# One hybrid diffusion step on one core: modulation matmuls kept in runs, and an opening stage that takes two output chunks a step

## Chip, core and metric

The kernel runs on one core of a Trainium2 chip. The time is device microseconds of one execution. PE is TensorE, DVE is VectorE, ACT is ScalarE, POOL is GpSimd, and SP issues most of the DMA.

## What is computed

Two layers run over 128 context tokens and 128 latent tokens, which the kernel carries side by side as 256 columns. Cut to what matters here:

```python
def _modulation(cond, w_mod, b_mod):
    m = jax.nn.silu(cond) @ w_mod + b_mod            # (2048) @ (2048, 6 * 2048)
    return [t[:, None, :] for t in jnp.split(m, 6, axis=-1)]

def _layer(x, mods, lw, ctx):
    shift1, scale1, gate1, shift2, scale2, gate2 = mods
    h = _rms_norm(x, lw['norm1_g']) * (1.0 + scale1) + shift1
    parts = _split_cols(h @ lw['w_in'])              # GLA, attention, DeltaNet heads
    mix = mixers(parts) @ lw['w_out']
    x = x + gate1 * mix
    h = _rms_norm(x, lw['norm2_g']) * (1.0 + scale2) + shift2
    ff = jnp.square(jax.nn.relu(h @ lw['w_ff1'])) @ lw['w_ff2']
    return x + gate2 * ff
```

There are two conditioning vectors (context and latent), so each of the six modulation slices of a layer is a product of a 2048 x 2048 float32 weight with two columns.

## The kernel before

Every weight comes from HBM in float32 tiles `raw` of 128 x 1024 (512 KB). For a dense product ACT rounds it to `hi` and DVE subtracts to get `lo`; PE then multiplies hi by the rounded activations `act`, hi by their remainder, and lo by the rounded part. The buffer of a `raw` comes free when `lo` is made. For a modulation slice no split is made: `sc`, the two conditioning columns, is the stationary operand, 32 columns wide, and the `raw` tile streams past it in float32. A float32 matmul is two instructions in the trace, so counts there are doubled. Since `sc` fills only 32 columns, four such matmuls go to the four column groups of the array (`tile_position=(0, 32 * gg)`), and each writes its own 32 rows of one PSUM bank.

`mod_pe` makes a slice outside the opening: 16 steps of two `raw` and four matmuls of 512 columns. Six slices go this way: 384 matmuls, or 96 groups of four. Four more slices are made on DVE (`mod_dv`), and slices 0 and 1 of layer 0 belong to the opening.

`first_phase` is the opening. It sums the squares of x on ACT and DVE, gets `rstd`, and then walks 16 output chunks n of 128. A chunk makes shift1 and scale1 for its 128 features: four `raw`, sixteen matmuls of 256 columns into the one bank of pool `pmod`, ACT copies it to `msb`, PE selects with `sel2` into a second tile of the same pool (`mod0t`), DVE adds the bias and makes `s12` and `ht`, and ACT and DVE write act[:, n]. For n below 8 the chunk of the input projection that act[:, n] allows is added to fourteen accumulators in seven PSUM banks (`fb`, `fbm`, `fbn`; weights `w_in0`, 896 columns a part). For n from 8 the step gives out a share of `half_jobs`: the first half of three more units (`HALF_D`, into `g`) and of three token units (`HALF_T`, into `gt`). All `raw` tiles of the opening come from the six buffers of pool `raw0`. After the opening the loop over `FIRST` adds the second half, with `raw` from the six buffers of `wraw`.

The order on each engine is not the order of the code. A scheduler simulates the program when it is built and writes a fixed order per engine; a token given to matmuls (`tok`) makes those that share it keep the order of the code among themselves. On the chip each engine goes through its order, and one instruction that waits holds all behind it. SP does the same with DMA issues.

Of the kernel before, what the change touches and what calls it, by code (L numbers as in the profile page):

```python
# [10 lines left out]
F32 = mybir.dt.float32  # L11
# [5 lines left out]
P = 128  # L17
# [1 line left out]
EPS = 1e-6  # L19
LEVELS = (16, 32, 64)  # L20
FIRST = (12, 0, 1, 2, 3, 4, 5, 6, 7, 8, 9, 10, 11, 13)
HALF_D = (14, 15, 16)
HALF_T = (0, 1, 2)
TB = 4
NRAW = 6
# [15 lines left out]
def tile_hybrid_step(ctx: ExitStack, tc: tile.TileContext, A: dict, O: dict):  # L41
# [381 lines left out]

    def mod_pe(l, m, modc, bm):
        ps = pmod.tile([P, 512], F32, tag="mod", name="mod")
        for k in range(16):
            raws = [load_half(A["w_mod"][l, m, k, half]) for half in range(2)]
            for gg in range(4):
                mm(
                    ps[32 * gg : 32 * gg + 32, :],  # L430
                    sc[:, 2 * k : 2 * k + 32],
                    raws[gg // 2][:, (gg % 2) * 512 : (gg % 2) * 512 + 512],
                    start=(k == 0),
                    stop=(k == 15),
                    tile_position=(0, 32 * gg),
                )
            yield
        msb = nrm.tile([P, 512], F32, tag="msb", name="msb")
        se.activation(msb, ps, AF.Copy)
        pt = ps  # L440
        for r in range(4):
            mm(pt[:, r * 8 : r * 8 + 8], msb[:, r * P : r * P + P], sel8)
        ve.tensor_tensor(
            modc[:, m].rearrange("p (g r) c -> p r g c", r=4),
            pt[:, 0:32].rearrange("p (r g c) -> p r g c", r=4, c=2),
            bc(bm[:, m].rearrange("p (g r) -> p r g", r=4), 2),
            ALU.add,
        )
        yield
# [16 lines left out]
    def get_rstd():  # L466
        st = pm.tile([P, 512], F32, tag="m", name="st")
        for g in range(2):
            mm(st[:, g : g + 1], sqacc[:, g * P : g * P + P], ones[:, 0:1])
        np_ = X["np"]  # L470
        v = np_.tile([P, 2], F32, tag="nv", name="nv")
        ve.tensor_scalar(v, st[:, 0:2], 1.0 / 2048.0, EPS, ALU.mult, ALU.add)
        rs = newton(np_, v, 2, "n2")
        b = bcast_cols(np_, rs, 2, "ht", 2)
        rstd = np_.tile([P, 256], F32, tag="rstd", name="rstd")
        se.activation(rstd, b[:, 0:256], AF.Copy)
        return rstd
# [70 lines left out]
    def first_phase(raw0):  # L548
        modc, s12, bm, ng = mods[0]
        X["np"] = raw0  # L550
        for n in range(16):
            accum_sq(n, n == 0)
        rate[0] = 0
        rstd = get_rstd()
        nb = len(FIRST)
        banks = [pg.tile([P, 512], F32, tag="g", name="fb") for _ in range(2)]
        banks += [pm.tile([P, 512], F32, tag="m", name="fbm") for _ in range(3)]
        banks += [pn.tile([P, 512], F32, tag="m", name="fbn") for _ in range(2)]
        tok = newtok()

        def half_jobs():
            for j in HALF_D:
                def evac(ps, j=j):
                    se.activation(part_of(j), gq3(ps), AF.Copy)

                yield from gemm_pieces(tsrc(A["w_in"][0], j), (0,), lambda k: act[:, k, 0:512], evac, raw0)
            for u in HALF_T:
                yield from gemm_tok(
                    lambda q, u=u: A["w_tok"][0][u, q], range(4),
                    lambda ps, g, u=u: se.activation(tok_dest(u, g), ps, AF.Copy), raw0,  # L570
                )

        jobs = half_jobs()
        njobs = 3 * len(HALF_D) + 12 * len(HALF_T)
        done = 0
        for n in range(16):
            ps = pmod.tile([P, 512], F32, tag="mod", name="mod0")
            for q in range(4):
                raw = load_half(A["w_mod0"][n, q], raw0)
                for kk in range(4):  # L580
                    mm(ps[32 * kk : 32 * kk + 32, 0:256], sc[:, 2 * (4 * q + kk) : 2 * (4 * q + kk) + 32], raw[:, kk * 256 : kk * 256 + 256],
                       start=(q == 0), stop=(q == 3), tile_position=(0, 32 * kk))
            msb = nrm.tile([P, 512], F32, tag="msb", name="msb")
            se.activation(msb[:, 0:256], ps[:, 0:256], AF.Copy)
            pt = pmod.tile([P, 512], F32, tag="mod", name="mod0t")
            for m in range(2):
                mm(pt[:, 2 * m : 2 * m + 2], msb[:, m * P : m * P + P], sel2)
            ve.tensor_tensor(
                modc[:, 0:2, n, :], pt[:, 0:4].rearrange("p (m c) -> p m c", m=2), bc(bm[:, 0:2, n], 2), ALU.add
            )  # L590
            ve.tensor_scalar(s12[:, 0, n, :], modc[:, 1, n, :], 1.0, ng[:, 0, n : n + 1], ALU.add, ALU.mult)
            t = X["np"].tile([P, 256], F32, tag="ht", name="ht", bufs=2)
            for g in range(2):
                s = slice(g * P, g * P + P)
                ve.scalar_tensor_tensor(t[:, s], X["x"][:, n, s], s12[:, 0, n, g : g + 1], rstd[:, s], ALU.mult, ALU.mult)
            h_chunk(n, t, modc[:, 0])
            if n >= 8:
                want = (n - 7) * njobs // 8
                while done < want:
                    next(jobs, None)  # L600
                    done += 1
                continue
            w = nb * 64
            for part in range(2):
                raw = raw0.tile([P, 1024], F32, tag="raw", name="raw")
                nc.sync.dma_start(raw[:, 0:w], A["w_in0"][n, part])
                hi = whi.tile([P, 1024], F32R, tag="hi", name="hi")
                lo = wlo.tile([P, 1024], F32R, tag="lo", name="lo")
                se.activation(hi[:, 0:w], raw[:, 0:w], AF.Copy)
                ve.tensor_tensor(lo[:, 0:w], raw[:, 0:w], hi[:, 0:w].bitcast(F32), ALU.subtract)  # L610
                for j in range(nb // 2):
                    u = part * (nb // 2) + j
                    o = banks[u // 2][:, (u % 2) * 256 : (u % 2) * 256 + 256]
                    h = hi[:, j * P : j * P + P]
                    l_ = lo[:, j * P : j * P + P]
                    kw = dict(tok=tok, skip_group_check=True)
                    mm(o, h, act[:, n, 0:256], start=(n == 0 and u % 2 == 0), stop=False, **kw)
                    mm(o, h, act[:, n, 256:512], start=False, stop=False, **kw)
                    mm(o, l_, act[:, n, 0:256], start=False, stop=(n == 7), **kw)
            if n == 7:  # L620
                for u, j in enumerate(FIRST):
                    src = gq3(banks[u // 2][:, (u % 2) * 256 : (u % 2) * 256 + 256])
                    if u % 4 < 2:
                        se.activation(part_of(j), src, AF.Copy)
                    else:
                        ve.tensor_copy(part_of(j), src)
        for _ in jobs:
            pass

# [9 lines left out]
    for l in range(L):  # L639
# [189 lines left out]

        def fill_gen():  # L830
            if l == 0:
                for j in HALF_D:
                    yield from gemm_pieces(wsrc(j), (1,), act_of, g_evac(j - 13))
            else:
                for j in range(4):
                    yield from gemm_pieces(wsrc(13 + j), (0, 1), act_of, g_evac(j))
            yield from tok_unit(0)
            marks.add("gv")
            for u in range(1, 4):
                yield from tok_unit(u)  # L840
            marks.add("akv")
            while "sg" not in lay:
                yield
            for h in GATES:
# [632 lines left out]
def _layout(inp):  # L1477
# [6 lines left out]
    D["cvec"] = c(cv.reshape(16, P, 2).transpose(1, 0, 2))  # L1484
    wm = inp["w_mod"]
    D["w_mod"] = c(wm.reshape(L, 16, P, 6, 2, 1024).transpose(0, 3, 1, 4, 2, 5))
    w0 = wm[0].reshape(4, 4, P, 6, 16, P)[:, :, :, 0:2]
    D["w_mod0"] = c(w0.transpose(4, 0, 2, 1, 3, 5).reshape(16, 4, P, 1024))
# [17 lines left out]
    nf = len(FIRST)  # L1506
    f0 = dcols[0].reshape(16, P, 25, P)[0:8, :, list(FIRST)]
# [137 lines left out]
```

## Time and profile before

| | |
|---|---|
| median of 3 runs | 2587.19 us (2587.05 to 2587.85) |
| the profiled execution | 2598.9 us, its span 2597.0 us |
| PE busy | 2522.5 us, 97% of the span |
| DVE busy | 1802.7 us, 69% |
| ACT busy | 1225.5 us, 47% |
| DMA | 611.83 MB, mean 236 GB/s |

The span is the time from the first to the last instruction of the profiled execution, and 1.9 us lie around it. The profiled execution is 11.7 us above the median of the runs. What differs between two kernels is worked out on the span and carried over to the median.

### The profile page before, as it was taken

How to read it: one execution, taken by the hardware profiler on the slowest of the kernel's cores; microseconds unless marked ns; L12 is line 12 of the kernel's file. 1: busy time of each engine (PE TensorE's matmuls, PEld its weight loads, DVE VectorE, ACT ScalarE, POOL GpSimd, SP SyncE). 2: the span in 40 equal slices, each digit the busy share in tenths (PEclk: the TensorE clock that was granted, in tenths of full speed). 3: DMA queues.
4: the chain of work that ended last, by engine and by line, in shares of the span. 5: the costliest groups of instructions: out<-in, count | busy, mean ns of one | idle time of the engine just before them, and what ended most of it. 6: DMA issues, size and time to landing. Idle time of an engine off the chain costs nothing. (4 is left out here: it accounts for less than half of the span.)

```text
span 2597.0 us, 47711 instructions
## 1 busy us (share of the span) xinstructions
PE 2522.5 (97%) x18988; PEld 2252.9 (87%) x18988; DVE 1802.7 (69%) x3197; ACT 1225.5 (47%) x1925; POOL 98.3 (4%) x121
## 2 busy tenths in 40 slices
PE   6999999999999999999999999999999999999999
PEld 4778677799988999899899888898999989999888
DVE  4457757668878767676766776697799865564665
ACT  3356244456444353344344663555565435445433
POOL 1000000003000000000001200000210000000000
PEclk9999999999999999999999999999999999999999
DMA  9966767776888877787877664445578766666664
GB/s 357 330 245 203 278 220 256 276 264 205 312 289 310 288 276 261 262 274 274 281 249 241 232 226 137 149 127 174 171 238 297 255 188 189 187 189 186 186 198 143
DMA packets 169551, 611.83 MB, mean 236 GB/s; under 512 B 19744, under 2 KB 20320, under 8 KB 169328
## 3 DMA queue, kind: packets, MB, share of 16 engines
q1 hardware_dynamic: 165024, 598.94, 68.7%
q0 software_dynamic: 2432, 6.61, 0.8%
q8 instruction: 149, 2.44, 0.4%
q10 hardware_dynamic: 1872, 3.23, 0.4%
q14 instruction: 74, 0.61, 0.1%
HBM read 602.41 MB, written 6.29 MB: 234 GB/s over the span
## 5 line engine op out<-in xcount | busy, mean ns | idle before, releaser
L55 ACT ACTIVATE hi<-raw 128x1024 fp32r<-128x1024 f32 (+1 forms) x742 | 784.1, 1057 | 1086.5 <-PE g L85 563.3
L55 DVE TENSOR_TENSOR lo<-raw,hi 128x1024 fp32r<-128x1024 f32 (+1 forms) x742 | 899.1, 1218 | 343.6 <-ACT hi L55 320.0
L85 PE MATMUL g<-act,hi 128*128 128x256 f32 (+1 forms) x7488 | 1056.7, 292 | 20.3 <-DVE x L55 8.0
L85 PEld LDWEIGHTS g<-act,hi 128*128 128x128 f32 x7488 | 955.4, 189 | 101.0 <-ACT hi L55 27.4
L85 PE MATMUL g<-act,lo 128*128 128x256 f32 x4000 | 562.4, 282 | 8.3 <-DVE lo L55 8.1
L85 PEld LDWEIGHTS g<-act,lo 128*128 128x128 f32 x4000 | 514.1, 189 | 24.1 <-DVE lo L55 11.8
L55 DVE SCALAR_TENSOR_TENSOR acc<-raw,sc,acc 128x1024 f32<-128x1024 f32 x240 | 299.5, 1281 | 142.8 <-DMA raw<-w_mod 141.6
L85 PE MATMUL g<-hid,hi 128*128 128x256 f32 (+1 forms) x1536 | 262.9, 320 | 3.2 <-DVE x L55 3.1
L55 DVE SCALAR_TENSOR_TENSOR x<-g,modc,x 128x128 f32<-128x128 f32 x448 | 142.0, 347 | 164.2 <-PE g L85 159.4
L85 PEld LDWEIGHTS g<-hid,hi 128*128 128x128 f32 x1536 | 217.7, 189 | 29.4 <-ACT hi L55 7.5
L85 PE MATMUL mod<-raw,sc 128*32 128x512 f32 (+1 forms) x1280 | 156.5, 527 | 22.7 <-DMA raw<-w_mod 18.0
L85 PE MATMUL gt<-hi,act 128*128 128x512 f32 x512 | 141.7, 409 | 3.3 <-ACT hi L55 3.2
L85 PE MATMUL g<-hid,lo 128*128 128x256 f32 x1024 | 142.9, 282 | 0.0
L85 PEld LDWEIGHTS g<-hid,lo 128*128 128x128 f32 x1024 | 135.6, 190 | 6.3 <-issue 0.8
L85 PEld LDWEIGHTS gt<-hi,act 128*128 128x128 f32 x512 | 94.3, 191 | 39.6 <-issue 11.1
L492 POOL TENSOR_TENSOR ht<-x,rstd 128x256 f32<-128x256 f32 x48 | 55.6, 1177 | 1006.9 <-ACT rstd L55 1003.2
L85 PEld LDWEIGHTS mod<-raw,sc 128*32 128x32 f32 x1280 | 31.3, 110 | 63.1 <-issue 17.1
L85 PE MATMUL gt<-lo,act 128*128 128x512 f32 x256 | 76.4, 407 | 0.0
L85 PE MATMUL gl<-hid,hi 128*128 128x258 f32 x384 | 70.4, 285 | 2.1 <-ACT hi L55 2.1
L85 PEld LDWEIGHTS gl<-hid,hi 128*128 128x128 f32 x384 | 59.3, 189 | 2.6 <-ACT hi L55 2.5
L85 PEld LDWEIGHTS gt<-lo,act 128*128 128x128 f32 x256 | 47.7, 191 | 12.7 <-issue 1.1
L85 PE MATMUL gl<-hid,lo 128*128 128x258 f32 x192 | 54.1, 284 | 0.8 <-DVE lo L55 0.7
(353 smaller groups left out, 1894.2 us busy)
## 6 DMA issues: line engine op xcount, KB each, us to landing
raw<-w_ff SPq DMA_DIRECT2D x512, 512.0 KB, 4.5
raw<-w_mod SPq DMA_DIRECT2D x384, 512.0 KB, 5.1
raw<-w_in SPq DMA_DIRECT2D x86, 512.0 KB, 4.3
raw<-w_tok SPq DMA_DIRECT2D x64, 512.0 KB, 4.5
raw<-w_out SPq DMA_DIRECT2D x64, 512.0 KB, 4.2
raw<-w_in SPq DMA_DIRECT2D x16, 448.0 KB, 6.1
x<-xT SPq DMA_DIRECT2D x8, 512.0 KB, 7.9
spill<-x ACTq DMA_DIRECT2D x4, 512.0 KB, 4.6
```

The lines of the kernel that those rows point to most:

```text
L55: return f(out, *a, **kw)
L85: i = nc.tensor.matmul(out, lhsT=lhsT, rhs=rhs, start=start, stop=stop, **kw)
L492: nc.gpsimd.tensor_tensor(t, X["x"][:, k, :], rstd, ALU.mult)
```

## The change

Three edits. In `mod_pe` the 64 matmuls of a slice share one token, and the column groups of a step are taken as 2, 3, 0, 1, so the first of the four needs the second of the two tiles. In `first_phase` the squares no longer go through a DVE sum: ACT writes the square of a chunk and PE adds it into `st` with two one-column matmuls per chunk. And the opening takes two output chunks a step: `mod_pair(j)` makes slices 0 and 1 for chunks 2j and 2j+1 with eight `raw` and sixteen matmuls of 512 columns, in the bank of `pmod` and one of `pn` in turn, and `mod_end(j)` finishes them. The accumulators are twelve instead of fourteen (`FB`), in six banks; units 11 and 13 go to `HALF_D`, which has five units now. The `w_in0` parts are 768 columns wide and come from `wraw`.

```diff
@@ mod_pe
+        tk = newtok()
-            for gg in range(4):
+            for gg in (2, 3, 0, 1):
                 mm(
                     ps[32 * gg : 32 * gg + 32, :],
                     ...
                     tile_position=(0, 32 * gg),
+                    tok=tk,
                 )
@@ first_phase
+        st = pn.tile([P, 512], F32, tag="m", name="st")
         for n in range(16):
-            accum_sq(n, n == 0)
+            t = raw0.tile([P, 256], F32, tag="sqt", name="sqt", bufs=2)
+            se.activation(t, X["x"][:, n, :], AF.Square)
+            for g in range(2):
+                mm(st[:, g : g + 1], t[:, g * P : g * P + P], ones[:, 0:1], start=(n == 0 and g == 0), stop=(n == 15),
+                   skip_group_check=True)
+        rstd = rstd_of(st)
+
+        def mod_pair(j):
+            ps = (pmod, pn)[j % 2].tile([P, 512], F32, tag=("mod", "m")[j % 2], name="mod0")
+            tk = newtok()
+            for q in range(4):
+                raws = [load_half(A["w_mod0"][j, q, h], raw0) for h in range(2)]
+                for kk in (2, 3, 0, 1):
+                    k = 4 * q + kk
+                    mm(ps[32 * kk : 32 * kk + 32, :], sc[:, 2 * k : 2 * k + 32], raws[kk // 2][:, (kk % 2) * 512 : (kk % 2) * 512 + 512],
+                       start=(q == 0), stop=(q == 3), tile_position=(0, 32 * kk), tok=tk)
+            return ps
+
+        def mod_end(j, ps):
+            msb = nrm.tile([P, 512], F32, tag="msb", name="msb")
+            se.activation(msb, ps, AF.Copy)
+            for u in range(4):
+                mm(ps[:, 2 * u : 2 * u + 2], msb[:, u * P : u * P + P], sel2)
...
+        pend = mod_pair(0)
...
+        for j in range(8):
+            mod_end(j, pend)
+            for n in (2 * j, 2 * j + 1):
...
+                h_chunk(n, t, modc[:, 0])
+            ready = pieces(2 * j) if j < 4 else None
+            if j < 7:
+                pend = mod_pair(j + 1)
+            if j < 4:
+                dense(2 * j, ready)
+                dense(2 * j + 1, pieces(2 * j + 1))
+            else:
+                want = (j - 3) * njobs // 4
+                while done < want:
+                    next(jobs, None)
+                    done += 1
```

On PE, in the part where the DeltaNet groups run beside the token units, before, with the last rows of one `mod_pe` step and the next one (`tb` are transposes, `gt` token units):

```order
L85 MATMUL mod<-raw,sc 32x512 x2
L85 MATMUL gt<-lo,act 128x512 x4
L85 MATMUL mod<-raw,sc 32x512
L94 MATMUL tb<-c_ident,Ns 128x128 x4
L85 MATMUL mod<-raw,sc 32x512
L94 MATMUL tb<-c_ident,Ns 128x128 x4
L85 MATMUL mod<-raw,sc 32x512 x4
```

And now, at the same transposes:

```order
L86 MATMUL gt<-lo,act 128x512 x4
L86 MATMUL mod<-raw,sc 32x512 x4
L95 MATMUL tb<-c_ident,Ns 128x128 x4
L86 MATMUL mod<-raw,sc 32x512 x4
L95 MATMUL tb<-c_ident,Ns 128x128 x4
```

A step that stood in three pieces stands in one. Over the whole program, outside the opening, the 384 matmuls form 113 groups of up to four different column groups before and 105 now; 96 would be whole.

On PE at the very start, before (`mod_249` is the first chunk's slice, `bcb` spreads `rstd` over the columns):

```order
L85 MATMUL mod_249<-raw,sc 32x256 x8
L85 MATMUL st<-c_ones,sqacc 128x1 x2
L85 MATMUL mod_249<-raw,sc 32x256 x8
L85 MATMUL mod0t<-c_sel_97,msb 128x2 x2
L85 MATMUL bcb<-diag,c_ones 128x256
L85 MATMUL fb<-act,hi 128x256 x2
```

And now (`mod_258` is the first pair, `mod_331` the second):

```order
L86 MATMUL st<-c_ones,sqt 128x1 x16
L86 MATMUL mod_258<-raw,sc 32x512 x4
L86 MATMUL st<-c_ones,sqt 128x1 x4
L86 MATMUL mod_258<-raw,sc 32x512 x4
L86 MATMUL st<-c_ones,sqt 128x1 x4
L86 MATMUL mod_258<-raw,sc 32x512 x4
L86 MATMUL st<-c_ones,sqt 128x1 x8
L86 MATMUL bcb<-diag,c_ones 128x256
L86 MATMUL mod_258<-raw,sc 32x512 x4
L86 MATMUL mod_258<-c_sel_97,msb 128x2 x4
L86 MATMUL mod_331<-raw,sc 32x512 x4
L86 MATMUL fb<-act,hi 128x256 x2
```

The first accumulator now stands behind eight `raw` instead of four, and behind 32 one-column matmuls instead of two.

On PE right after the last accumulator of the opening, before (`mod_1101` is the slice of chunk 10):

```order
L85 MATMUL mod_1007<-raw,sc 32x256 x4
L85 MATMUL g<-act,hi 128x256 x16
L85 MATMUL g<-act,lo 128x256 x8
L85 MATMUL g<-act,hi 128x256
L85 MATMUL mod0t<-c_sel_97,msb 128x2 x2
L85 MATMUL g<-act,hi 128x256 x15
L85 MATMUL g<-act,lo 128x256 x6
L85 MATMUL mod_1101<-raw,sc 32x256 x16
```

And now (`mod_784`, `mod_935` and `mod_1118` are pairs 4, 5 and 6):

```order
L86 MATMUL mod_784<-raw,sc 32x512 x4
L86 MATMUL mod_784<-c_sel_97,msb 128x2 x4
L86 MATMUL mod_935<-raw,sc 32x512 x16
L86 MATMUL g<-act,hi 128x256 x16
L86 MATMUL mod_935<-c_sel_97,msb 128x2 x4
...
L86 MATMUL g<-act,lo 128x256 x8
L86 MATMUL mod_1118<-raw,sc 32x512 x16
L86 MATMUL mod_1118<-c_sel_97,msb 128x2 x4
```

A run of sixteen matmuls needed four `raw` before and needs eight now.

## Rows read from the trace of the kernel before

**Rows 1.** The page's first part: busy time, share of span, instructions.

```profile
PE 2522.5 (97%) x18988; PEld 2252.9 (87%) x18988; DVE 1802.7 (69%) x3197; ACT 1225.5 (47%) x1925; POOL 98.3 (4%) x121
```

**Rows 2.** Windows: stretch, its length, busy us by engine, clock, DMA share, GB/s.

```profile
core 0: us, PE busy (x) PEld busy (x) DVE busy (x) ACT busy (x) POOL busy (x), PEclk, DMA share, GB/s
0.00:25.00 25.00, 7.35 (x42) 3.12 (x42) 12.38 (x38) 10.59 (x23) 9.44 (x21) 1.00 0.92 338
25.00:42.00 17.00, 12.37 (x95) 9.09 (x96) 4.20 (x10) 3.57 (x8) 0.00 (x0) 0.85 1.02 403
42.00:101.60 59.60, 54.97 (x527) 44.48 (x527) 25.96 (x54) 20.73 (x37) 0.00 (x0) 0.98 0.94 339
101.60:173.20 71.60, 64.61 (x477) 47.01 (x473) 33.27 (x71) 29.37 (x52) 0.00 (x0) 0.95 0.78 288
173.20:400.00 226.80, 226.80 (x1497) 172.84 (x1498) 163.68 (x459) 104.70 (x174) 5.83 (x10) 1.00 0.68 233
```

**Rows 3.** Timeline of PE and DVE to the first accumulator: start, length, instruction, idle before.

```profile
12.91 1.08 PE L85 MATMUL mod<-raw,sc 128*32 128x256 f32 x8 [12.91 <-DMA raw<-w_mod]
...
15.27 1.01 PE L85 MATMUL st<-c_ones,sqacc 128*128 128x1 f32 x4
...
22.99 0.15 DVE L55 TENSOR_TENSOR modc<-mod0t,bm 128x4 f32<-128x4 f32 x1
...
23.32 1.08 DVE L55 TENSOR_TENSOR lo<-raw,hi 128x896 fp32r<-128x896 f32 x1
...
25.45 0.97 PE L85 MATMUL fb<-act,hi 128*128 128x256 f32 x2 [2.21 <-ACT act L55]
```

**Rows 4.** PE timeline at a split modulation step, then at a whole one.

```profile
276.20 1.05 PE L85 MATMUL mod<-raw,sc 128*32 128x512 f32 x2
277.18 0.66 PE L94 MATMUL tb<-c_ident,Ns 128*128 128x128 f32 x4
...
279.32 1.07 PE L85 MATMUL mod<-raw,sc 128*32 128x512 f32 x8
```

**Rows 5.** PE timeline of the opening's second half: one unit, one token quarter.

```profile
109.81 2.04 PE L85 MATMUL g<-act,hi 128*128 128x256 f32 x16
...
112.64 0.50 PE L85 MATMUL mod0t<-c_sel,msb 128*128 128x2 f32 x4
...
122.28 1.98 PE L85 MATMUL gt<-hi,act 128*128 128x512 f32 x8
...
125.09 1.93 PE L85 MATMUL mod<-raw,sc 128*32 128x256 f32 x32
```

**Rows 6.** PE timeline late in the opening.

```profile
151.00 0.64 PE L85 MATMUL mod<-raw,sc 128*32 128x256 f32 x8 [1.12 <-DMA raw<-w_mod]
...
154.63 3.78 PE L85 MATMUL gt<-hi,act 128*128 128x512 f32 x8
```

**Rows 7.** Window just behind it, columns as in the windows above.

```profile
154.00:160.00 6.00, 5.86 (x16) 4.66 (x16) 3.80 (x8) 2.21 (x4) 0.00 (x0) 0.50 1.01 392
```

**Rows 8.** PE timeline of one step of the opening, chunk 4.

```profile
66.67 0.61 PE L85 MATMUL mod0t<-c_sel,msb 128*128 128x2 f32 x4 [0.50 <-ACT msb L55]
67.53 1.50 PE L85 MATMUL mod<-raw,sc 128*32 128x256 f32 x24 [0.26 <-DVE modc L55]
68.97 0.72 PE L85 MATMUL fb<-act,hi 128*128 128x256 f32 x2
...
74.41 0.64 PE L85 MATMUL mod<-raw,sc 128*32 128x256 f32 x8
75.61 0.27 PE L85 MATMUL mod0t<-c_sel,msb 128*128 128x2 f32 x1 [0.56 <-ACT msb L55]
```

**Rows 9.** DMA issues from 0 to 175 us: count, KB each, median us to landing.

```profile
raw<-w_mod SPq DMA_DIRECT2D x64, 512.0 KB, 6.7
raw<-w_in SPq DMA_DIRECT2D x12, 512.0 KB, 9.3
```

**Rows 10.** DMA issues of the whole span, from the page.

```profile
raw<-w_tok SPq DMA_DIRECT2D x64, 512.0 KB, 4.5
```

More of the change, by code (lines that the diff above doesn't have):

```diff
@@ L21 @@
 FIRST = (12, 0, 1, 2, 3, 4, 5, 6, 7, 8, 9, 10, 11, 13)
-HALF_D = (14, 15, 16)
+FB = (12, 0, 1, 2, 3, 4, 5, 6, 7, 8, 9, 10)
+HALF_D = (11, 13, 14, 15, 16)
 HALF_T = (0, 1, 2)
@@ L469, in get_rstd, with rstd_of @@
             mm(st[:, g : g + 1], sqacc[:, g * P : g * P + P], ones[:, 0:1])
+        return rstd_of(st)
+    def rstd_of(st):
         np_ = X["np"]
@@ L550, in first_phase @@
         X["np"] = raw0
+        rate[0] = 0
+        nb = len(FB)
+        st = pn.tile([P, 512], F32, tag="m", name="st")
         for n in range(16):
-            accum_sq(n, n == 0)
-        rate[0] = 0
-        rstd = get_rstd()
-        nb = len(FIRST)
+            t = raw0.tile([P, 256], F32, tag="sqt", name="sqt", bufs=2)
[19 more added lines that the diff above has]
+                mm(ps[:, 2 * u : 2 * u + 2], msb[:, u * P : u * P + P], sel2)
+            js = slice(2 * j, 2 * j + 2)
+            ve.tensor_tensor(
+                modc[:, 0:2, js, :], ps[:, 0:8].rearrange("p (n m c) -> p m n c", n=2, m=2), bc(bm[:, 0:2, js], 2), ALU.add
+            )
+            ve.scalar_tensor_tensor(
+                s12[:, 0, js].rearrange("p k c -> p c k"), modc[:, 1, js].rearrange("p k c -> p c k"), 1.0,
+                ng[:, 0, js].unsqueeze(1).to_broadcast([P, 2, 2]), ALU.add, ALU.mult,
+            )
+        pend = mod_pair(0)
         banks = [pg.tile([P, 512], F32, tag="g", name="fb") for _ in range(2)]
         banks += [pm.tile([P, 512], F32, tag="m", name="fbm") for _ in range(3)]
-        banks += [pn.tile([P, 512], F32, tag="m", name="fbn") for _ in range(2)]
+        banks += [pn.tile([P, 512], F32, tag="m", name="fbn")]
         tok = newtok()
@@ L575, in first_phase, with pieces @@
         done = 0
[L576 to L603, printed above, removed]
+        w = nb * 64
+        def pieces(n):
+            out = []
             for part in range(2):
-                raw = raw0.tile([P, 1024], F32, tag="raw", name="raw")
+                raw = wraw.tile([P, 1024], F32, tag="raw", name="raw")
                 nc.sync.dma_start(raw[:, 0:w], A["w_in0"][n, part])
@@ L610, in first_phase, with dense @@
                 ve.tensor_tensor(lo[:, 0:w], raw[:, 0:w], hi[:, 0:w].bitcast(F32), ALU.subtract)
+                out.append((hi, lo))
+            return out
+        def dense(n, his):
+            for part, (hi, lo) in enumerate(his):
                 for j in range(nb // 2):
@@ L619, in first_phase @@
                     mm(o, l_, act[:, n, 0:256], start=False, stop=(n == 7), **kw)
-            if n == 7:
-                for u, j in enumerate(FIRST):
+        for j in range(8):
+            mod_end(j, pend)
+            for n in (2 * j, 2 * j + 1):
+                t = raw0.tile([P, 256], F32, tag="ht", name="ht", bufs=2)
+                for g in range(2):
+                    s = slice(g * P, g * P + P)
+                    ve.scalar_tensor_tensor(t[:, s], X["x"][:, n, s], s12[:, 0, n, g : g + 1], rstd[:, s], ALU.mult, ALU.mult)
+                h_chunk(n, t, modc[:, 0])
[10 more added lines that the diff above has]
+                    done += 1
+            if j == 3:
+                for u, jj in enumerate(FB):
                     src = gq3(banks[u // 2][:, (u % 2) * 256 : (u % 2) * 256 + 256])
                     if u % 4 < 2:
-                        se.activation(part_of(j), src, AF.Copy)
+                        se.activation(part_of(jj), src, AF.Copy)
                     else:
-                        ve.tensor_copy(part_of(j), src)
+                        ve.tensor_copy(part_of(jj), src)
         for _ in jobs:
@@ L831, in fill_gen @@
             if l == 0:
-                for j in HALF_D:
+                for j in (14, 15, 16):
                     yield from gemm_pieces(wsrc(j), (1,), act_of, g_evac(j - 13))
@@ L1486, in _layout @@
     D["w_mod"] = c(wm.reshape(L, 16, P, 6, 2, 1024).transpose(0, 3, 1, 4, 2, 5))
-    w0 = wm[0].reshape(4, 4, P, 6, 16, P)[:, :, :, 0:2]
-    D["w_mod0"] = c(w0.transpose(4, 0, 2, 1, 3, 5).reshape(16, 4, P, 1024))
+    w0 = wm[0].reshape(4, 2, 2, P, 6, 8, 2, P)[:, :, :, :, 0:2]
+    D["w_mod0"] = c(w0.transpose(5, 0, 1, 3, 2, 6, 4, 7).reshape(8, 4, 2, P, 1024))
     D["bmod"] = c(inp["b_mod"].reshape(L, 6, 16, P).transpose(0, 3, 1, 2))
@@ L1505, in _layout @@
     D["w_in"] = dunits(dcols)
-    nf = len(FIRST)
-    f0 = dcols[0].reshape(16, P, 25, P)[0:8, :, list(FIRST)]
+    nf = len(FB)
+    f0 = dcols[0].reshape(16, P, 25, P)[0:8, :, list(FB)]
     D["w_in0"] = c(f0.reshape(8, P, 2, nf * 64).transpose(0, 2, 1, 3))
```

## The prediction

> **What bounds the kernel now.** The page's first line comes first: PE is busy 97% of the span, 2522.5 us, so only 74.5 us of PE idle can be won, plus whatever PE does at a bad rate [rows 1]. The windows tell where the idle lies: 17.65 us of it in the first 25 us, 4.6 up to 42, 4.6 up to 101.6 and 7.0 up to 173.2, where the loop over FIRST begins. From there to 400 us it is zero [rows 2]. So the opening holds 34 us of idle, and behind it a microsecond of PE work is a microsecond of time. In the opening the DMA moves 338 to 403 GB/s while PE starves, and in 42 to 101.6 PE is nearly full; the first accumulator starts at 25.45 us [rows 2, 3].
>
> The timeline of PE shows bad rates of two kinds. A piece of a modulation step that is one matmul (two instructions) costs 0.98 us from its start to the next instruction, and a run of eight instructions, four matmuls, is busy 1.07 us [rows 4]. So a step in two pieces costs twice. And the granted clock falls to 0.50, 1.2 instead of 2.4 GHz, for 6 us after some idle late in the opening: eight instructions that take 1.98 us take 3.78 [rows 5, 6, 7].
>
> **mod_pe in one run.** Outside the opening the 384 matmuls form 113 groups before and 105 now, by the order of PE. Each group fewer saves 0.98 us [rows 4]: 8 x 0.98 = 7.8 us. All the affected stretches but one or two are without idle [rows 2], so I take all of it: -7.8 us. The bounds are 0 (a split hides under a wait) and -8.6 at the 1.07 us of a run. What the new column order adds is a wait for the second tile ahead of the first; behind it on PE would stand dense work, but from 173.2 to 400 us PE waits for nothing, so its tiles have landed, and I cost it at 0.
>
> **The opening, up to the first accumulator.** Before, it stood behind four raw; now behind eight, and SP issues six w_in0 parts between the sixth and the seventh. Until the eighth has landed the DMA must move x (2.1 MB), eight raw (4.2), six parts of 128 x 768 (2.4) and about 1.5 MB of constants: 10.2 MB. It moved 8.45 MB by 25 us and then 403 GB/s [rows 2], so the eighth lands at 25 + 1.75/0.403 = 29.3 us. Then follow, at the low clock that PE has there: the last four matmuls, 2.2 us (1.08 for the half width [rows 3]); the msb copy, 0.6 (0.50 of idle before [rows 8]); four selecting matmuls, 2.0 (as the one-column ones, 1.01 for two [rows 3]); and the second pair's first group, 2.2, under which the 1.4 us of DVE and ACT work hide (25.45 - 22.99 less the 1.08 of a lo between [rows 3]). That is 36.3: the first accumulator starts near 36 us instead of 25.45. The thirty-two one-column matmuls cost 16 us at the low clock, but they start as soon as x lands and wait for nothing but ACT. The last two squares stand on ACT behind three hi roundings whose tiles land near 25 us, so rstd is there near 32, not last. Range for this point: 33 to 40.
>
> **The pairs.** One step before, from selection to selection, is 66.67 to 75.61 = 8.94 us, of it 5.44 us fourteen accumulators, 0.389 each [rows 8]. Two steps are 17.9. A pair has 24 x 0.389 = 9.3, four groups of 0.98, two 0.5 us selections, one wait for msb of 0.6 and 0.4 that the next pair's first group doesn't hide: 15.2. The step before, less the four accumulators that move, is 17.9 - 1.6 = 16.3, so a pair gains 1.1 us, from half the waits. With 2.5 us lost to the low clock at the start (0.85 over 17 us is 5.1 us at half rate [rows 2]), the last accumulator ends at 36 + 2.5 + 3 x 15.2 + 9.3 + 2.0 = 95.4 us, against 101.6, where [rows 2] are cut. A pair needs 5.8 MB, 380 GB/s, which the 403 of [rows 2] allow. The Trainium skill, "DMA: Bandwidth & Descriptors", in "Where 436 GB/s comes from", gives some 358 GB/s as the HBM side's limit for a core. The 403 GB/s held for 17 us speaks against it here; by the rule a pair takes 16.1 us and the forecast rises by 2.7 us.
>
> **The rest of the opening.** Work left then: thirteen groups (12.8 us), four pairs' selections at 1.0, five units and twelve token quarters at 2.85 (2.83 and 2.81 [rows 5]) = 48.5: 65.3 us. Now the waits. Pairs 5 and 6 each stand as one run of sixteen matmuls that needs eight raw, but raw0 has six buffers. The seventh and eighth are issued when the run's own first group has freed theirs. From issue to landing I take 4.5 us, the median of token tiles over the whole span [rows 10], since the queue is empty then; 6.7 is the opening's median [rows 9]. For pair 5 that gives idle of 2.0 and 1.8 us before its third and fourth group, and 1.4 before the first unit, whose tile comes behind and must be rounded; for pair 6 3.8 and 0.7; for pair 7, spread among token quarters, 2.2. Sum 12 us. Before, a run needed four raw, and the whole stretch idled 7.0 us [rows 2]. Three waits of about 0.5 to 1.1 us were followed there by 6 us at 0.50 [rows 6, 7], which costs 3.0; I count one such drop for each of the two runs: 6 us. The loop over FIRST then starts at 95.4 + 65.3 + 12 + 6 = 178.7 us instead of 173.2: +5.5. SP is in order, so whatever is queued behind a held raw (the parts from wraw, later the token tiles) is held with it; that is in the walk. DVE loses fifteen adds of the squares and ACT nothing; neither was last.
>
> **Sum.** 2597.0 - 7.8 + 5.5 = 2594.7 us of span, 2.3 less. Carried to the median of 2587.19: 2584.9, say 2585. Orders elsewhere are reshuffled up to 700 us; I give that 0, plus or minus 3.
>
> **Rivals.** First, *the deeper prefetch wins*: the waits of the two runs don't come. Then the late part idles and loses clock as before, 7.0 + 3: 95.4 + 65.3 + 10 = 170.7, which is -2.5; with -7.8, 2577 (2572 to 2581). For it speaks that twelve buffers feed the early part instead of six; against it that the runs need eight from six. A landing faster than 4.5 would do it. The Trainium skill, "DMA: Bandwidth & Descriptors", in "Anatomy of one DMA", puts a transfer at about 2.0 us plus its bytes at 436 GB/s, an estimate of 3.2 us for 512 KB; the traces show 4.5 to 9.3 [rows 9, 10], so I give that rule little.
>
> Second, *the six-buffer ring makes it slower*: the raw of the two runs land as late as the opening's tiles do now. Four waits hang on a landing L, so the time moves by 4 x (L - 4.5). It is slower by more than 0.2% (5.2 us, about what a measurement of this kernel tells from no change) from L = 4.5 + (5.2 + 2.3)/4 = 6.4. The opening's median of 6.7 [rows 9] is just past that, though it was taken with a full queue. At L = 7 it is +7.7: 2595.
>
> Third, *the runs don't do what they say*: a split costs nothing in the end, because what comes next would have waited anyway. Then only +5.5 stays: 2592.7. The zero idle from 173.2 to 400 [rows 2] speaks against it.
>
> **Chances and range.** The forecast has 0.42, from 2580 to 2590, of which 0.05 lie more than 5.2 us below; the first rival 0.30, the second 0.20, the third 0.08, half of it beyond the bound. That is 0.35 faster, 0.41 within 0.2%, 0.24 slower. The range from 2574 to 2597 takes in most of both rivals and the 33 to 40 of the first accumulator.
>
> **What the new profile would show.** The first accumulator near 36 us and the last ending near 95; nearly whole runs of eight instructions behind the opening, and a PE that still doesn't idle from the opening to 400 us; in 95 to 125 us two runs of modulation matmuls broken by waits for raw of 2 to 4 us, with the clock near 0.5 behind them; the loop over FIRST starting near 179. Wrong would be: an opening that ends before 172, with no such waits (first rival); one that ends after 183 (second); idle on PE in the DeltaNet part, waiting for w_mod tiles, which I put at zero.

## The result and the profile after

The changed kernel takes 2603.64 us (median of 4 runs, 2601.1 to 2610.82), the kernel before beside it 2587.52 (2587.05 to 2588.17): 1.0067 times as long, interval 1.0045 to 1.0089. It is slower by 16.1 us where 2.3 less were forecast.

The two profiled executions hardly show this: their spans are 2599.2 and 2597.0 us. The one of before lay 11.7 us above its median, the one of after at the low end of its runs. Single executions of one kernel scatter by some 8 us either way here, so the verdicts below rest on many runs and the profiles on stretches that repeat.

The page's first part (busy us, share, instructions), to be put beside [rows 1]:

```profile
PE 2527.1 (97%) x18792; PEld 2257.4 (87%) x18792; DVE 1790.3 (69%) x3168; ACT 1222.9 (47%) x1919; POOL 97.3 (4%) x121
```

PE has 196 instructions fewer and is busy 4.6 us longer. The same windows as [rows 2] (stretch, length, busy us by engine, clock, DMA share, GB/s):

```profile
0.00:25.00 25.00, 15.79 (x72) 11.06 (x72) 1.44 (x5) 8.22 (x18) 9.47 (x21) 1.00 0.92 338
25.00:42.00 17.00, 13.38 (x60) 8.74 (x57) 7.11 (x26) 4.51 (x11) 0.00 (x0) 1.00 0.99 383
42.00:101.60 59.60, 55.08 (x411) 40.67 (x410) 21.54 (x47) 18.16 (x33) 0.00 (x0) 0.94 0.91 339
101.60:173.20 71.60, 61.02 (x354) 42.28 (x354) 28.41 (x57) 26.05 (x45) 0.00 (x0) 0.86 0.79 287
173.20:400.00 226.80, 222.13 (x1466) 174.09 (x1464) 155.09 (x414) 105.93 (x175) 5.00 (x8) 1.00 0.65 217
```

Two rows differ in kind. From 101.6 to 173.2 PE idles 10.6 us instead of 7.0, at a clock of 0.86 instead of 0.95. And from 173.2 to 400, where it idled not at all, it now idles 4.7 us, 1.5 of them still in the opening.

Up to the first accumulator, PE's timeline (start, length, instruction, idle before) beside [rows 3]:

```profile
14.89 1.93 PE L86 MATMUL mod<-raw,sc 128*32 128x512 f32 x8
16.75 1.87 PE L86 MATMUL st<-c_ones,sqt 128*128 128x1 f32 x8
19.83 1.93 PE L86 MATMUL mod<-raw,sc 128*32 128x512 f32 x8 [1.22 <-DMA raw<-w_mod]
21.70 1.87 PE L86 MATMUL st<-c_ones,sqt 128*128 128x1 f32 x8
23.49 1.93 PE L86 MATMUL mod<-raw,sc 128*32 128x512 f32 x8
25.36 3.58 PE L86 MATMUL st<-c_ones,sqt 128*128 128x1 f32 x16
31.81 1.22 PE L86 MATMUL bcb<-diag,c_ones 128*128 128x256 f32 x2 [2.88 <-DVE diag L56]
32.96 1.94 PE L86 MATMUL mod<-raw,sc 128*32 128x512 f32 x8
...
39.31 1.00 PE L86 MATMUL fb<-act,hi 128*128 128x256 f32 x2
```

The first accumulator starts at 39.3 us instead of 25.45. ACT in the same stretch tells why the squares end late:

```profile
15.05 0.42 ACT L56 ACTIVATE sqt<-x 128x256 f32<-128x256 f32 x1 [0.45 <-PE st L86]
17.86 0.42 ACT L56 ACTIVATE sqt<-x 128x256 f32<-128x256 f32 x1 [2.39 <-PE st L86]
...
22.80 0.42 ACT L56 ACTIVATE sqt<-x 128x256 f32<-128x256 f32 x1 [3.67 <-PE st L86]
...
27.32 0.42 ACT L56 ACTIVATE sqt<-x 128x256 f32<-128x256 f32 x1 [0.44 <-PE st L86]
```

Each square waits for PE to have used one of two buffers, and PE's sums stand between modulation groups that wait for tiles. So the last square is written at 27.3 us, `diag` follows 4 us later, and `bcb`, which stands ahead of the fourth group on PE, holds it.

Behind the last accumulator, pair 5 and pair 6 on PE, beside [rows 5, 6]:

```profile
104.83 1.06 PE L86 MATMUL mod<-raw,sc 128*32 128x512 f32 x8
106.91 1.94 PE L86 MATMUL mod<-raw,sc 128*32 128x512 f32 x8 [1.00 <-DMA raw<-w_mod]
110.18 1.94 PE L86 MATMUL mod<-raw,sc 128*32 128x512 f32 x8 [1.34 <-DMA raw<-w_mod]
112.75 1.94 PE L86 MATMUL mod<-raw,sc 128*32 128x512 f32 x8 [0.63 <-DMA raw<-w_mod]
115.85 3.78 PE L86 MATMUL g<-act,hi 128*128 128x256 f32 x16 [1.17 <-ACT hi L56]
...
129.96 2.78 PE L86 MATMUL mod<-raw,sc 128*32 128x512 f32 x24
135.95 1.06 PE L86 MATMUL mod<-raw,sc 128*32 128x512 f32 x8 [3.21 <-DMA raw<-w_mod]
...
186.95 2.16 PE L86 MATMUL g<-act,hi 128*128 128x256 f32 x16 [0.71 <-ACT aq L56]
```

and the windows behind the two runs:

```profile
108.00:119.00 11.00, 7.86 (x34) 3.56 (x31) 2.46 (x3) 3.54 (x4) 0.00 (x0) 0.50 1.00 347
136.00:143.00 7.00, 6.20 (x32) 5.29 (x33) 4.22 (x8) 4.24 (x6) 0.00 (x0) 0.57 1.03 413
```

The waits and the fall to 0.50 come where they were forecast. The seventh and eighth tile of pair 5 are issued at 105.9 us, when the run's first group (104.83 us, 1.06 long) has freed theirs; those of pair 6 at 131.1, behind its first group too. DMA issues at the two points, with KB each and median us to landing:

```profile
raw<-w_mod SPq DMA_DIRECT2D x2, 512.0 KB, 5.9
raw<-w_mod SPq DMA_DIRECT2D x2, 512.0 KB, 4.0
```

The loop over FIRST starts at 186.95 us, not 173.2.

### The profile page after: what moved, and what is told of

It reads as the page before. It is cut to its first block, busy times and chain, and to the rows that moved or that the text cites. A ratio compares the mean times of both kernels' runs of the same rounds, so it can differ in the third digit from the quotient of the medians.

```text
span 2599.2 us, 47233 instructions
## 1 busy us (share of the span) xinstructions
PE 2527.1 (97%) x18792; PEld 2257.4 (87%) x18792; DVE 1790.3 (69%) x3168; ACT 1222.9 (47%) x1919; POOL 97.3 (4%) x121
## 4 chain that ended last, share of the span: by engine, by line
PE 46%; DVE 2%; DMA 2%; issue 1%; ACT 1%; POOL 0%; DVEq 0%; SPq 0%; ACTq 0%; POOLq 0%
PE g L86 37%; PE gt L86 3%; DMA raw<-w_mod 1%; PE gl L86 1%; PE mod L86 1%; DVE lo L56 1%; DVE act L56 0%; DVE acc L56 0%; PE ga L86 0%; PE eb L86 0%; ACT hi L56 0%; DMA raw<-w_in 0%; PE scb L86 0%; PE oatb L86 0%; PE ob L86 0%
## 5 line engine op out<-in xcount | busy, mean ns | idle before, releaser
L86 PE MATMUL mod<-raw,sc 128*32 128x512 f32 x1024 | 151.0, 632 | 8.7 <-DMA raw<-w_mod 8.7
L86 PEld LDWEIGHTS mod<-raw,sc 128*32 128x32 f32 x1024 | 22.5, 110 | 40.5 <-DMA raw<-w_mod 15.8
```

Of the source, the lines that this page charges most:

```text
L86: i = nc.tensor.matmul(out, lhsT=lhsT, rhs=rhs, start=start, stop=stop, **kw)
```

## The experiments

Four marks are read from each profile: the start of the first accumulator, the end of the last, the start of the loop over FIRST, and the time from there to the first matmul of `gl`, which contains the first three slices of `mod_pe`. "Groups" counts groups of the six slices in the order of PE. The ratio is to the kernel before in the same series, with its 95% interval.

| kernel | groups | first acc. | last acc. ends | FIRST | FIRST to gl | ratio |
|---|---|---|---|---|---|---|
| before (first profile) | 113 | 25.5 | 101.1 | 173.2 | 414.5 | |
| before_again | 113 | 25.1 | 100.8 | 171.8 | 417.3 | 1.0001 [0.9988, 1.0013] |
| after (first profile) | 105 | 39.3 | 102.1 | 186.95 | 414.2 | 1.0067 [1.0045, 1.0089] |
| after_again | 105 | 38.3 | 102.0 | 185.1 | 418.3 | 1.0060 [1.0047, 1.0074] |
| modpe_only | 105 | 24.9 | 100.3 | 169.4 | 416.7 | 1.0005 [0.9995, 1.0015] |
| opening_only | 113 | 37.2 | 102.2 | 186.6 | 414.9 | 1.0036 [1.0024, 1.0048] |
| opening_dve_squares | 113 | 36.5 | 101.8 | 189.0 | 414.2 | 1.0030 [1.0018, 1.0043] |
| opening_raw8 | 113 | 36.1 | 97.0 | 175.5 | 414.2 | 0.9998 [0.9983, 1.0012] |
| opening_dve_raw8 | 113 | 31.1 | 98.2 | 178.7 | 414.3 | 0.9996 [0.9985, 1.0006] |
| opening_spread | 113 | 38.4 | 103.2 | 180.7 | 415.5 | 1.0023 [1.0010, 1.0037] |
| opening_spread_raw8 | 113 | 36.3 | 100.3 | 173.5 | 414.3 | 0.9990 [0.9976, 1.0003] |
| before_raw8 | 113 | 25.1 | 101.2 | 166.0 | 414.5 | 0.9971 [0.9958, 0.9983] |
| before_raw8_again | 113 | 25.3 | 101.1 | 166.3 | 414.5 | 0.9973 [0.9958, 0.9988] |
| squares_pe_raw8 | 113 | 35.3 | 106.5 | 170.9 | 414.8 | 0.9967 [0.9953, 0.9981] |
| modpe_raw8 | 105 | 25.2 | 101.4 | 166.2 | 412.2 | 0.9991 [0.9979, 1.0004] |
| after_raw8 | 105 | 36.5 | 99.3 | 173.3 | 417.7 | 1.0014 [1.0001, 1.0027] |
| order_slice1_raw8 | 115 | 25.3 | 101.4 | 166.3 | 421.8 | 0.9991 [0.9978, 1.0004] |
| order_slice3_raw8 | 109 | 25.2 | 101.3 | 166.1 | 411.3 | 0.9969 [0.9957, 0.9981] |

**The two halves apart.** `modpe_only` is the kernel before with the new `mod_pe`:

```diff
+        tk = newtok()
-            for gg in range(4):
+            for gg in (2, 3, 0, 1):
+                    tok=tk,
```

> Only the token and the column order in mod_pe, on the kernel before; 105 groups instead of 113. Theory opening (the whole loss is in the opening, the runs of mod_pe save their 0.98 us each): 7.8 us faster, 2580. Rival (the reshuffled order behind the opening eats the saving, or the wait for the second tile costs): 2585 or more.

`opening_only` is the changed kernel with these lines undone.

> The new opening with mod_pe as before; 113 groups outside the opening. Theory opening: slower than the whole change by the 7.8 us of mod_pe, 2604 + 8 = 2612, loop over FIRST near 187 us. Rival (the opening costs only the few us that the walk gave, the rest of the loss is elsewhere): 2593.

`before_again` and `after_again` repeat both kernels beside them.

> The kernel before, unchanged, to see how one profiled execution stands to the timed ones. The first profile of it stood at 2598.9 us against a median of 2587.5. If that profile showed an unusual execution, this profile will stand near 2587 and the opening will end earlier than 173.2 us in it. If a profiled execution is always longer by some 12 us, it will stand near 2599 again with the opening ending near 173.

> The changed kernel, unchanged: 2601 to 2611 us so far in four runs. Theory opening: the loop over FIRST starts near 187 us again and the spread of the times comes from the clock after the two modulation runs that wait for raw. Rival: the opening is the same in all executions and the spread lies elsewhere.

The opening alone costs 0.0036, about 9 us; its 2598.8 us lie between the 2612 and the 2593 expected. The new `mod_pe` alone gives nothing where 7.8 us were forecast (2591.1 us, as its rival had it). The second profile of the kernel before stands at 2592.1 us, 4.1 above the median of its runs. In the order of PE the token by itself moves nothing; the column order by itself makes all of the 105 groups.

**Where the saved groups went.** From 195 to 640 us, windows of before, `modpe_only` and after:

```profile
195.00:640.00 445.00, 441.64 (x3164) 350.60 (x3162) 314.53 (x815) 214.93 (x390) 32.78 (x40) 1.00 0.71 241
195.00:640.00 445.00, 430.23 (x3133) 347.33 (x3132) 312.34 (x812) 211.25 (x390) 32.77 (x40) 1.00 0.71 241
195.00:640.00 445.00, 435.62 (x3185) 355.30 (x3184) 314.03 (x824) 211.45 (x378) 32.82 (x40) 1.00 0.70 239
```

PE idles 3.4, 14.8 and 9.4 us. Of what it waits for in `modpe_only`, tiles are 3.0 us, and more is waited for what ACT and DVE make (us in total, times, longest):

```profile
PE mod L85 <- DMA raw<-w_mod: 3.0, 3, 1.6
PE g L85 <- ACT hi L55: 2.4, 3, 1.4
PE g L85 <- DVE x L55: 2.1, 1, 2.1
...
PE qkb L85 <- ACT E L55: 1.5, 1, 1.5
...
PE oatb L85 <- ACT pT L55: 1.3, 1, 1.3
```

In the first profile of before none of the waits for w_mod, x, E and pT appears there; in `before_again` there is one for w_mod, 0.9 us. One of the waits for w_mod is at the very step of [rows 4], 3 us earlier in this kernel:

```profile
272.94 1.06 PE L85 MATMUL mod<-raw,sc 128*32 128x512 f32 x8
273.94 0.66 PE L94 MATMUL tb<-c_ident,Ns 128*128 128x128 f32 x4
276.23 1.06 PE L85 MATMUL mod<-raw,sc 128*32 128x512 f32 x8 [1.63 <-DMA raw<-w_mod]
277.22 0.66 PE L94 MATMUL tb<-c_ident,Ns 128*128 128x128 f32 x4
```

The three pieces of before stood ahead of, between and behind other work. As one run the step costs two pieces less, 1.96 us, and 1.63 of it come back as a wait for the second tile.

**The squares and the ring.** Two edits on `opening_only`, apart and together (`opening_dve_squares`, `opening_raw8`, `opening_dve_raw8`), and the ring on the kernel before (`before_raw8`):

```diff
-NRAW = 6
+NRAW = 8
...
-            for g in range(2):
-                mm(st[:, g : g + 1], t[:, g * P : g * P + P], ones[:, 0:1], ...)
+            accum_sq(n, n == 0)
-        rstd = rstd_of(st)
+        rstd = get_rstd()
```

> The new opening with mod_pe as before, and with the squares summed on DVE as before. Theory: the squares run through two buffers, so ACT and PE take turns and rstd comes at about 33 us; on PE the matmul that spreads it stands ahead of the fourth group of the first pair and holds it 2.9 us. Without that the first accumulator starts at 34 to 36 us instead of 37.2 to 39.3, the loop over FIRST 2 to 4 us earlier than 186.6, and the ratio to the kernel before goes from 1.0036 to about 1.0025. Rival: the eighth tile of the pair lands near 33 us anyway; then the first accumulator stays at 37 to 39 and the ratio at 1.0036.

> The new opening with mod_pe as before, and with eight buffers in the opening's ring instead of six. Theory: the runs of pairs 5 and 6 wait for their seventh and eighth tile because the ring has six; with eight the waits of 1.0, 1.3, 0.6 and 3.2 us go and most of the 6 us at half clock with them, the loop over FIRST starts at 176 to 180 us instead of 186.6, and the ratio goes from 1.0036 to 0.999 to 1.001. Rival: the DMA is the limit there, not the ring; then the waits move by a tile but stay, FIRST starts at 183 to 187 and the ratio is 1.003 to 1.004.

> Both of the two edits before. If both theories hold, FIRST starts at 173 to 177 us, about where it does before, and the ratio is 0.997 to 1.000. If the first accumulator alone moves, FIRST starts near 183; if the ring alone, near 178. If neither, 186 to 187 and 1.0036.

> The kernel before with eight buffers in the opening's ring. Theory: the same ring causes the waits for tiles late in the old opening (7.0 us of idle and some 3 us of half clock between 101.6 and 173.2); FIRST starts 3 to 8 us earlier than 171.8 to 173.2, ratio 0.997 to 0.999. Rival: with four tiles a chunk six buffers are enough and the waits are the DMA's; FIRST starts within 1.5 us of before, ratio 0.9995 to 1.0005.

Without the sums on PE the first accumulator moves by 0.7 us only, and the rival looks right; FIRST, expected 2 to 4 us earlier, starts 2.4 us later. PE of `opening_dve_squares`, then of `opening_dve_raw8`, at the third and fourth group of the first pair:

```profile
21.78 1.94 PE L86 MATMUL mod<-raw,sc 128*32 128x512 f32 x8
30.20 1.94 PE L86 MATMUL mod<-raw,sc 128*32 128x512 f32 x8 [6.48 <-DMA raw<-w_mod]
```

```profile
22.06 1.70 PE L86 MATMUL mod<-raw,sc 128*32 128x512 f32 x8
24.54 1.06 PE L86 MATMUL mod<-raw,sc 128*32 128x512 f32 x8 [0.78 <-DMA raw<-w_mod]
```

and what SP issues in each (start, length, transfers):

```profile
2.60 5.99 SPq L208 DMA_DIRECT2D raw<-w_mod  x6
8.82 10.25 SPq L613 DMA_DIRECT2D raw<-w_in  x6
20.63 5.39 SPq L208 DMA_DIRECT2D raw<-w_mod  x6
```

```profile
2.63 8.19 SPq L208 DMA_DIRECT2D raw<-w_mod  x8
12.56 9.71 SPq L613 DMA_DIRECT2D raw<-w_in  x6
```

With six buffers the seventh tile is issued behind six w_in0 parts, at 20.6 us, and the fourth group starts at 30.2. With eight it goes out with the others and the group starts at 24.5. On six buffers, then, the eighth tile (30.2 us) and `bcb` (30.7 to 31.8) each held the fourth group. With eight and the sums on PE (`opening_raw8`) the group runs at 26.1, ahead of `bcb`, and the first accumulator waits for rstd itself, until 36.1. Only both edits together bring it to 31.1.

These 5 us are not handed on. From the first accumulator to the end of the last `opening_dve_raw8` takes 67.2 us at a granted clock of 0.88, `opening_raw8` 60.9 at 0.97. FIRST starts at 178.7, what was expected of the ring alone, 3.2 us later than with the sums on PE, and the ratios are level (0.9996 and 0.9998).

On the new opening the two buffers are worth what was expected: `opening_raw8` reaches FIRST at 175.5 us instead of 186.6 and is 0.0038, some 10 us, faster, level with the kernel before. Only 5.9 of the 11.1 us at FIRST lie behind the last accumulator, where idle falls from 12.4 to 7.8 us; the half clock that was expected to go with it stays (granted clock 0.90 and 0.91). On the old opening the ring is worth 5.5 to 7 us up to FIRST and 0.0029 of the time, as the theory had it.

So the ring of six explains little of the difference between the two openings. It is 0.0036 with six buffers and still 0.0027 with eight (2587.95 against 2581.69 us in one series), and at FIRST 13.4 to 14.8 us and 9.5; what the ring takes off the ratio, 0.0009, is within the intervals. The window of `before_raw8` late in the opening, beside the fourth of [rows 2]:

```profile
101.60:166.00 64.40, 61.84 (x476) 44.77 (x472) 32.52 (x70) 28.12 (x50) 0.00 (x0) 1.00 0.81 302
```

2.6 us of idle, and the clock never falls. The new opening with eight buffers idles 7.8 us behind its last accumulator, in 78.5 us instead of 64.9; two units more, 5.7 us by the forecast's price, are in that.

**The runs of sixteen.** `opening_spread` takes `opening_only` and hands out the four groups of pairs 5 to 7 among the units, `opening_spread_raw8` does so with eight buffers:

```diff
-                pend = mod_pair(j + 1)
-                while done < want:
-                    next(jobs, None)
+                for i in range(4):
+                    next(qs, None)
+                    want = d0 + (i + 1) * ((j - 3) * njobs // 4 - d0) // 4
+                    while done < want:
+                        next(jobs, None)
```

> The new opening with mod_pe as before and six buffers; the four groups of pairs 5 to 7 are spread among the units and token quarters instead of standing as one run of sixteen matmuls. Theory: the late loss comes from runs that need eight tiles out of a ring of six; spread, the waits of 1.8, 1.5, 0.8, 3.4 and 1.4 us and most of 6 us at half clock go, the late part (last accumulator to the loop over FIRST) takes 71 to 76 us instead of 84.4, and the ratio falls from 1.0036 to 1.000 to 1.001. Rival: the DMA's rate holds the tiles wherever they stand; then the waits move to other places and the late part stays at 82 to 85 us.

> The same spread with eight buffers. The late part was 78.5 us with eight buffers and whole runs. If what is left there (waits of 2.9 and 2.2 us and the clock at 0.90) comes from the runs too, it falls to 70 to 73 us, FIRST starts at 167 to 170 and the ratio is 0.996 to 0.998, level with the old opening on eight buffers (0.9971). If pairs cost more than that, it stays above 0.998.

The late part (last accumulator to FIRST) falls from 84.4 to 77.5 us: the waits inside the runs are gone (for w_mod 0.8 us instead of 7.5), and the granted clock is 0.98 instead of 0.90. It missed the 71 to 76, and the ratio of 1.0023 missed 1.000 to 1.001: waits for `hi` grew from 1.8 to 5.7 us, the longest in front of the first unit, whose tile now comes later:

```profile
105.98 1.07 PE L86 MATMUL mod<-raw,sc 128*32 128x512 f32 x8
109.22 3.06 PE L86 MATMUL g<-act,hi 128*128 128x256 f32 x16 [2.17 <-ACT hi L56]
```

With eight buffers the late part is 73.1 us against 78.5 for whole runs. FIRST starts at 173.5 and the ratio is 0.999, both above the expected 167 to 170 and 0.996 to 0.998: at an equal ring the new opening still starts FIRST 7.4 us later than the old one (166.0). What that is was not taken apart. The sums on PE cost 4.6 us at FIRST in the old opening (`squares_pe_raw8`, below), but on the new one, with whole runs, FIRST came 2.4 and 3.2 us later without them.

**mod_pe on the better ring.** `modpe_raw8` and `after_raw8` are `modpe_only` and the changed kernel with eight buffers.

> The new mod_pe on the old opening with eight buffers. Theory: the eight groups saved come back as waits behind the opening, whatever the opening is: ratio as the old opening on eight buffers, 0.9971, give or take 0.001, with some 10 us less PE busy and some 10 us more idle from 195 to 640 us. Rival: the missing gain was only scatter between executions; then 0.994 to 0.9955.

> The changed kernel with eight buffers in the opening's ring. If ring and mod_pe are independent: the changed kernel's 1.006 less the 0.0038 that the ring was worth on the new opening alone, 1.002. If the new mod_pe costs nothing by itself: 1.000. A value below 0.998 would say that the ring was hiding a gain of mod_pe.

The new `mod_pe` takes away most of what the ring gives: 0.9991, above both expected ranges, against 0.9971 and 0.9973. On the new opening it is 1.0014 against 0.9998, between the two values expected. With the 1.0060 against 1.0036 beside them, three of four pairs put its cost at 0.0016 to 0.0024, the fourth at 0.0005. Two of the pairs lie within one series. `modpe_only` is 1.1 us above the kernel before, inside the scatter; all six runs of `after_again` (2600.5 to 2609.3 us) lie above all five of `opening_only` (2596.6 to 2600.4), by 6.1 us in the median. That it gains is not borne out anywhere.

**One slice at a time.** On `before_raw8` the column order is changed in the first or in the third slice only:

```diff
+        columns = (2, 3, 0, 1) if X["slices"] == 1 else range(4)
-            for gg in range(4):
+            for gg in columns:
```

> The old opening with eight buffers once more, as the base of the three runs beside it and because it is the fastest so far: 0.9971 [0.9958, 0.9983] before, so 0.996 to 0.998 again, with the loop over FIRST starting at 166 us, and 3 to 5 us of PE idle from 195 to 640 us.

> The old opening with eight buffers; the column order 2, 3, 0, 1 in the first slice of mod_pe only. The order on PE then has 17 groups for the first slice instead of 20, but 28 instead of 20 for the third, 115 in all. If a split costs its 0.98 us, this is 2 us slower than the base beside it. If a split stands in for a wait and costs nothing, it is level with the base, within 1.5 us, with PE busier and less idle behind the first slice.

> The same with the order in the third slice only: 16 groups for it instead of 20, 109 in all, the first two slices as before. If a split costs its 0.98 us, 4 us faster than the base (ratio lower by 0.0015). If the saved groups come back as waits, level with the base or slower, with about 4 us less busy and 4 us or more of new idle between 400 and 560 us and none before 400.

The price of a group holds here: with four groups fewer in slice 3 the stretch from the end of the second slice to that of the third takes 93.4 us instead of 97.4, four times 0.98, though with 1.1 us of new idle. From FIRST to `gl` 3.2 us are left of it, and in the ratio nothing is seen (0.9969 beside 0.9973); PE idles 25 us from 640 to 1400, against 16.5 and 18.8 of its base.

The first slice shows where a saving goes. From FIRST to the end of that slice, where its selecting matmuls start, all twelve profiles with the old order in it take 158.6 us and PE never idles. The six with the new order have three groups fewer, 2.9 us, and take 158.2 to 160.4, with 1.8 to 3.9 us of idle. `before_raw8`, then `order_slice1_raw8` at the end of the slice (FIRST at 166.03 and 166.27):

```profile
324.64 0.96 PE L85 MATMUL mod<-c_sel,msb 128*128 128x8 f32 x8
```

```profile
325.34 0.96 PE L85 MATMUL mod<-c_sel,msb 128*128 128x8 f32 x8
```

and the two waits of `order_slice1_raw8` in it:

```profile
232.19 1.16 PE L85 MATMUL qkb<-dqk 128*128 128x128 f32 x8 [1.30 <-ACT E L55]
271.75 1.06 PE L85 MATMUL mod<-raw,sc 128*32 128x512 f32 x8 [1.47 <-DMA raw<-w_mod]
```

All six wait at these two places, 1.0 to 1.7 us for E and 0.3 to 1.6 for the second tile. Behind the slice the scheduler orders the rest anew in `order_slice1_raw8` (20 and 28 groups in slices 2 and 3 instead of 23 and 20), and the stretch to `gl` is 7.3 us longer, 4.7 of it new idle up to 560 us. Its median is 4.8 us above its base in the same series, where 2 us, or a level time, had been expected. So the new order of the first slice is enough to bring the waits; which of the later ones come from the new order behind it was not isolated.

**The squares alone.** `squares_pe_raw8` is `before_raw8` with the squares summed on PE.

> The old opening with eight buffers, with the squares summed on PE as in the change. On the new opening the sum on PE and the tiles of the first pair ended within 2 us of each other, so neither alone was seen. Here four tiles land by 20 us and rstd decides: on the new opening it came at 33 us against 24 in the old one, so the first accumulator starts at 30 to 34 us instead of 25.1, and the loop over FIRST 4 to 9 us later than 166 (ratio 0.998 to 1.000). Rival: PE kept at work by the squares reaches its higher clock earlier and wins that back; then FIRST starts at 165 to 168.

The first accumulator starts at 35.3 us, 10 us later and just past the 30 to 34 expected. Half of it is won back before the last accumulator (71.2 us between the two instead of 76.0, with 6.3 us of idle instead of 10.1), and FIRST starts 4.6 us later, as expected. But the ratio is no higher, 0.9967, where 0.998 to 1.000 was expected. From `gl` to the end the nine profiles with the new opening take 1991 to 2001 us, 1997 in the mean, and the nine with the old one 1998 to 2009, 2003 in the mean. Some of a head start seems to be given back there, where PE waits for `lo`, `hi` and `x`; no run tried that by itself.

## Why the prediction was wrong

*mod_pe, -7.8 us: wrong, and the larger miss.* The price was right: 0.98 us a group is what slice 3 gives back. The step that failed is "from 173.2 to 400 us PE waits for nothing, so its tiles have landed, and I cost it at 0". With three groups fewer in the first slice PE waits in that very stretch, 0.3 to 1.6 us for a second tile and 1.0 to 1.7 for E, and the slice takes 158.2 to 160.4 us instead of 158.6. Zero idle in the old order says that nothing came later than its use there; it doesn't say how much earlier it came. A second term at nothing without a reason is "Orders elsewhere are reshuffled up to 700 us; I give that 0": waits for x and pT came up behind the first slice, and whether this brings them or the order of slices 2 and 3 is open. In the five profiles with the order changed in all slices PE idles 9 to 15 us from 195 to 640, in those with the old order 2.5 to 5. The third rival, "a split costs nothing in the end, because what comes next would have waited anyway", was the right one and had a chance of 0.08.

*The first accumulator, 36: 39.3, at the upper end of its range.* The steps that failed are that the sums "wait for nothing but ACT" and that rstd is "not last". The squares took turns with PE through two buffers, behind groups that waited for tiles; rstd was there at 33.5, and by the order of PE `bcb` stood ahead of the fourth group, so the tiles' work waited for it too. The tile's time, 29.3 by bytes, came out near (30.2, where nothing else holds the group). It rests on the six w_in0 parts ahead of it: with eight buffers the tile goes out before them and the group starts at 24.5. The term itself bears little on the time: 5 us less of it (`opening_dve_raw8`) and 10 us more (`squares_pe_raw8`) left the ratio where it was.

*The pairs, 15.2 each: 16.1 at best.* In `opening_raw8` a pair takes 65.25 to 81.33; waits of 0.65, 0.20 and 0.74 stand there instead of 0.6 and 0.4, and groups cost 1.0 to 1.06. With some more half clock than counted the last accumulator ends at 102.1 instead of 95.4: 3.3 from the start, 3.4 from the pairs. The 16.1 that the Trainium skill's rule gave ("DMA: Bandwidth & Descriptors", "Where 436 GB/s comes from") is met in number, but those waits are for ACT and DVE, none for a transfer, and from the first accumulator to the last `opening_raw8` moves 381 GB/s.

*The rest of the opening, 83.3: 84.9.* The mechanism was right: the last two tiles of a run go out when its first group frees theirs, and `opening_raw8` and `opening_spread` bear it out. That the idle is 12.0 us against 12 is in part luck. The six waits that were forecast come to 9.0 us (3.0, 1.2, 3.2 and 1.6 for pair 5, its unit, pair 6 and pair 7), though pair 5's last six tiles took 4.7 to 6.6 us to land where 4.5 was taken; waits of 3.1 us for msb and aq, which were not counted, fill the sum. The half clock came behind both runs, but for 13.7 and 6.8 us instead of 6 each.

So up to FIRST the change costs 13.8 us by the profiles instead of 5.5: 3.3, 3.4 and 1.6 for the three parts. By the medians the opening alone costs about 9. The other 4 to 5 seem to be given back behind `gl`, where profiles with the new opening are 6 us shorter in the mean; the cause is open.

*The sum.* -7.8 + 5.5 became about 1 + 9 with each alone, and 15.5 to 17.3 together. The 5 to 7 us more than the sum of the two lie just within the intervals: the new `mod_pe` costs 6.1 us on the new opening and about 1 on the old one, and why is open. The second rival had the sign and a part of the mechanism (the ring). Its condition, landings of over 6.4 us, was not met: 5.9 and 4.0 us for the last tiles of pairs 5 and 6, and the idle was as forecast. The rule beside the first rival (the Trainium skill, "DMA: Bandwidth & Descriptors", "Anatomy of one DMA") is written for transfers that GpSimd issues. SP issues these, and the fastest in pairs 5 and 6 took 3.6 us.

## What to carry to other kernels

Zero idle on the bounding engine is a property of the order that was profiled: before removing a filler, look for what it ran beside, and price the wait that stands bare without it. Before a stage is given larger steps, count the buffers that one step needs against its ring; here two more buffers gained where the whole change lost (2581.69 us against 2587.57, and 2584.07 against 2591.65 when repeated: faster than both kernels of this case). And try such a cure on the kernel before as well: with eight buffers the new opening is level with the kernel before, but 6.3 us behind the old opening that has them too. Where two things end within 2 us of each other, an experiment that removes one shows little: remove both, and follow what that gains to the end, since here 5 us at the first accumulator were gone by the last.

## What the runs showed of the hardware

On the way to the first accumulator a group of four 512-column matmuls takes 1.93 us (14.89 to 33 us above), the same as at 110 us with the clock at 0.50, though the windows up to 42 us give the granted clock as 1.00; later it takes 1.06. The record of the granted clock doesn't show that early slow stretch.

In `opening_dve_squares` the window from 25 to 42 us gives 0.60, and the groups in it take 1.93 to 1.94 us as well. So the two windows differ in what they record and not in how fast PE was, and a clock of 1.00 before the first fall in a record is not evidence of a fast PE.
